# A two-layer encoder trunk: the second layer's memory keys and values move into that layer, and its mixer's input is transposed through DRAM

## The chip, the core and the metric

The kernel runs on one core of a Trainium2 chip. TensorE (PE in the profile) multiplies matrices; VectorE (DVE) and ScalarE (ACT) do the elementwise work and empty the accumulators; GpSimd (POOL) takes reciprocal square roots and a little setup; SyncE (SP) issues most transfers. Each engine works through its own list of instructions in the order in which the program was built, and waits where an instruction needs something that is not there yet. The metric is the time of the whole program in microseconds (us); lower is better.

## The reference

The input is one sequence of 256 frames with 1024 features, and a memory of 256 rows with 1024 features. Two layers follow each other. Each layer does the following in float32:

```
x = x + 1/2 * SwiGLU_1(RMSNorm(x))                      # FFN of 2816 units ("ffn 1")
h = RMSNorm(x);  q_s, k_s, v_s, q_m = split(h @ w_in)   # "mixer" begins
k_m, v_m = split(RMSNorm(mem) @ w_mem_kv)               # memory keys and values, 1024 -> 2*256
o_m = attention of q_m (4 heads of 64) over k_m, v_m
o_s = layer 0: chunked attention with a learned relative bias, 12 heads
      layer 1: differential attention with rotary positions, 6 heads
x = x + concat(o_s, o_m) @ w_out                        # mixer ends
x = x + 1/2 * SwiGLU_2(RMSNorm(x))                      # "ffn 2"
```

The memory keys and values of a layer depend on `mem` and on that layer's weights alone, not on `x`. So they can be made at any time before that layer's memory attention.

## The kernel before

Precision comes from a split: each float32 operand is written as hi + lo, where hi is the operand rounded to the matmul's input type, and a product is three matmuls (hi times hi, hi times lo, lo times hi) that add into one accumulator. The helper `dense` issues these three (L516, L519, L522). A weight chunk of 128x2048 comes from DRAM into one of 3 `raw` buffers; ScalarE casts it to `hi` in four pieces (L341), VectorE subtracts to get `lo` in four pieces (L359), and 4 pairs of hi and lo are held at a time. A chunk of the projection weights or of the memory weights then serves 24 matmuls of 512 columns.

The left operand has to be transposed, with features on partitions. Two ways are in the kernel. `prep_half` transposes four 128x128 blocks on TensorE (L552, tile `xtp`) and multiplies by the norm's gain out of the accumulator (L586). `prep_dram` uses none of TensorE: VectorE transposes 32x32 blocks (L597, `xb`), ScalarE's queue writes them to a DRAM scratch `xd` (L603) and reads them back in another order (L610, `xr4`), and VectorE multiplies by the gain (L616, `y`). Behind both, `prep_rest` casts on ScalarE (L624, `xh`) and subtracts on VectorE (L628, `xl`). This is done for two row blocks (tb) of 128 rows, in two halves (hf) of 512 features each. `finish` adds the accumulator to x (L668) and then starts one of the two ways; in the kernel before, only the end of ffn 1 in layer 0 takes the DRAM way.

The memory is transposed once, into a DRAM scratch `md`. `memory_prep` reads it back (L1043, four tiles `mr`) and makes, for each layer and each of 8 feature blocks kk, `memh` on ScalarE (L1106) and `meml` on VectorE (L1110, two instructions). `memory_kv` then multiplies these with `w_mem_kv` (tile `kv`, 48 matmuls for one layer), takes the head norm of the keys, and sends them through DRAM once more (`kd`, `kr`). In the kernel before, both layers' `memh`, `meml`, `kv` and their weights come at the start of layer 0's mixer: 96 matmuls stand between the last down projection of ffn 1 (tile `acc`) and the first input projection (tile `pj`).

What sets the order is a planner in the program, run when it is built. The class `Flow` holds a clock and the times at which it thinks that ScalarE, VectorE and GpSimd come free; each piece of work is a generator that yields a time or a condition. `split_hi` and `split_lo` go on when their engine is free within 0.4 us, or when their chunk is the one that TensorE is at (`calm_a`, `calm_v`). `memory_prep` goes on only where its engine is free at that very time:

```
yield lambda: flow.free["A"] <= flow.now
nc.scalar.activation(hi, src, AF.Copy, scale=g)
```

The planner's times are not measured ones; what it leaves is an order for each engine. The names in an order carry numbers, since a name such as `hi` has a new tile for every chunk.

Of the kernel before, what the change touches and what calls it, by code (L numbers as in the profile page):

```python
# [27 lines left out]
KT = D // P  # L28
# [6 lines left out]
GC_FFN1, GC_MIX, GC_MEM, GC_FFN2 = 0, 16, 32, 48  # L35
# [107 lines left out]
def kernel(  # L143
# [10 lines left out]
    nc = tc.nc  # L154
    PSUM = bass.MemoryType.PSUM
    NRAW, NHL, NT2 = 3, 4, 19
    flow = Flow()
# [12 lines left out]
    g4 = Slots(flow, gp, "g", 12)  # L170
# [44 lines left out]
    gcol = const.tile([P, NGC], F32, name="gcol")  # L215
# [67 lines left out]
    def add_chunk(parts, uses=8, w=1):  # L283
        return Item([add_raw(parts)], uses, w)
# [102 lines left out]
    plan = {}  # L387
# [102 lines left out]

    for l in range(DEPTH):
        plan_ffn(l, 1, ffn1_w_gate, ffn1_w_up, ffn1_w_down)
        if l == 0:
            for ll in range(DEPTH):
                plan[ll, "kv"] = [add_chunk(cols4(w_mem_kv[ll], c, 0, 512, 0)) for c in range(2)]
        plan[l, "in"] = []
        for blk in WI:
            ids = []
            for c in range(2):
                o, parts = 0, []  # L500
                for c0, n in blk:
# [184 lines left out]
    def ffn(l, nm, xt, gc_next):  # L686
# [251 lines left out]
        acc = Acc()  # L938
# [33 lines left out]
        for c in range(SPLIT):  # L972
            prog[0] = c
            if c in sv:
                if c == sv[0]:
                    flow.until(banks.has(4))
                    ms = [bank(f"m{j}", (P, 512)) for j in (1, 5, 6, 7)]
                t = seven(c, ms)
                if c == sv[-1]:
                    flow.spawn(seven_sums(ms, t))  # L980
                continue
            for k in range(2):
                for tb in range(2):
                    for hf in range(2):
                        down(c, k, tb, hf)
            g4.give()
            if (l, nm) == (0, 1) and c == 2:
                flow.spawn(memory_prep())
        if nm == 1:
            table_hint(AF.Exp)  # L990
        assert xt_room[0]
        xt_room[0] = False
        nxt = None if gc_next is None else Xt(nm == 2 and PAIR[l + 1, 1] is not None)
        for tb in range(2):
            flow.spawn(finish(acc, tb, nxt, gc_next, True, (l, nm) == (0, 1)))
# [34 lines left out]
    memT = {}  # L1030
# [55 lines left out]
        for tb in range(2):  # L1086
            yield from rsqrt(mrs[tb], s2[:, tb:tb + 1], 1, 1.0 / D)

    def memory_prep():
        yield lambda: len(memd) == 4 and g2.left >= 8  # L1090
        rs = []
        for q in range(4):
            rs.append(from_dram(memd[q], "mr"))
            yield flow.now + 1.0
        yield flow.now + 4.0
        for l in range(DEPTH):
            yield g4.has(4)
            mh, ml = ([g4.take([P, 4, SEQ], F32R, f"{n}{l}{i}") for i in range(2)] for n in ("memh", "meml"))
            tt = [None] * KT
            memT[l] = (mh, ml, tt)  # L1100
            for kk in range(KT):
                src = rs[kk // 2][:, :, :, kk % 2, :].rearrange("p a t j -> p t a j")
                g = gcol[:, GC_MEM + l * KT + kk:GC_MEM + l * KT + kk + 1]
                hi, lo = (m[kk // 4][:, kk % 4, :].rearrange("p (t a j) -> p t a j", t=2, a=4) for m in (mh, ml))
                yield lambda: flow.free["A"] <= flow.now
                nc.scalar.activation(hi, src, AF.Copy, scale=g)  # L1106
                yield flow.act(256)
                yield lambda: flow.free["V"] <= flow.now
                for tb in range(2):
                    nc.vector.scalar_tensor_tensor(out=lo[:, tb], in0=src[:, tb], scalar=g, in1=hi.bitcast(F32)[:, tb],  # L1110
                                                   op0=ALU.mult, op1=ALU.subtract)
                    tt[kk] = flow.dve(128, 0.06)
        g2.give(4)

    def split_evac(dst, src, gain):
# [186 lines left out]
    def mixer(l, xt, gc_next):  # L1302
# [518 lines left out]
```

## Time and profile before

| What | Value |
|---|---|
| Time, median of 3 runs (lowest to highest) | 950.66 us (949.93 to 950.89) |
| Span of the profiled execution, first to last instruction | 948.2 us |
| PE busy | 940.9 us, 99% of the span |
| VectorE, ScalarE, GpSimd busy | 828.6, 590.4, 110.0 us |
| Read from and written to DRAM | 190.04 and 15.20 MB |

The span lies 2.46 us under the median of the runs; the profile gives no other time of its own execution, so these 2.46 us stand for what lies around the span. A matmul's busy time runs to its modelled end and overlaps the next one's, so the distance between two starts is the number to use: 0.227 us for 128x512. In the timeline view a row gives start, length, engine, line, operation and names; equal rows that follow each other are merged, with x and their count.

### The profile page before, as it was taken

Reading aid. Unit: us, or ns where it says so; the run is one execution under the profiler, and the core shown is the slowest. Engines: PE = TensorE matmul, PEld = TensorE weight load, DVE = VectorE, ACT = ScalarE, POOL = GpSimd, SP = SyncE. Lnnn points to the kernel's source line nnn. Section 1 sums busy time; section 2 is a strip of 40 time slices with the busy share of each in tenths; the row PEclk is TensorE's granted clock in tenths of the full one; section 3 lists DMA queues with packets and bytes.
Section 4 is the critical chain, followed back from the end, with each engine's and each line's share of the span. In section 5 each row is a group of like instructions: output and inputs, shape, how many; then the busy total and the mean of one; then the engine's idle time right before and its main releaser. Section 6 shows DMA issues by size and latency. Waiting matters only on the chain. (4 is left out here: it accounts for less than half of the span.)

```text
span 948.2 us, 13317 instructions
## 1 busy us (share of the span) xinstructions
PE 940.9 (99%) x4456; PEld 772.1 (81%) x4456; DVE 828.6 (87%) x1501; ACT 590.4 (62%) x1126; POOL 110.0 (12%) x160
## 2 busy tenths in 40 slices
PE   9999999999999999999999999999999999999998
PEld 7888888887777888888888888888887788888887
DVE  6989988888787899989889899796989899998995
ACT  6656666677676756647546656563777765655671
POOL 1000038731210100000000000000434100000000
PEclk9999999999999999999999999999999999999999
DMA  9878799787525387887746679775632467589561
GB/s 296 271 229 252 227 332 307 244 268 250 178 90 178 106 258 224 266 285 219 244 146 216 224 222 295 241 248 166 216 119 82 133 215 229 183 258 331 175 226 48
DMA packets 172574, 206.13 MB, mean 217 GB/s; under 512 B 10265, under 2 KB 147290, under 8 KB 172506
## 3 DMA queue, kind: packets, MB, share of 16 engines
q1 hardware_dynamic: 169498, 202.92, 66.6%
q10 hardware_dynamic: 3008, 2.37, 0.8%
q8 instruction: 35, 0.57, 0.3%
q14 instruction: 33, 0.27, 0.1%
HBM read 190.04 MB, written 15.20 MB: 216 GB/s over the span
## 5 line engine op out<-in xcount | busy, mean ns | idle before, releaser
L341 ACT CAST hi<-raw 128x512 fp32r<-128x512 f32 (+1 forms) x466 | 335.1, 770 | 161.5 <-DMA raw<-in_ffn_w_up_dram 40.8
L359 DVE TENSOR_TENSOR lo<-raw,hi 128x512 fp32r<-128x512 f32 (+1 forms) x466 | 392.0, 875 | 32.9 <-ACT hi L341 32.6
L519 PE MATMUL gu<-lo,xh 128*128 128x512 f32 x528 | 205.5, 389 | 0.5 <-DVE lo L359 0.5
L522 PE MATMUL gu<-hi,xl 128*128 128x512 f32 x528 | 205.8, 390 | 0.0
L516 PE MATMUL gu<-hi,xh 128*128 128x512 f32 x528 | 205.6, 389 | 0.0
L522 PEld LDWEIGHTS gu<-hi,xl 128*128 128x128 f32 x528 | 99.1, 188 | 21.3 <-DVE xl L628 0.9
L519 PEld LDWEIGHTS gu<-lo,xh 128*128 128x128 f32 x528 | 99.1, 188 | 21.3 <-DVE lo L359 0.9
L516 PEld LDWEIGHTS gu<-hi,xh 128*128 128x128 f32 x528 | 99.1, 188 | 20.6 <-ACT xh L624 0.2
L522 PE MATMUL acc<-hi,ht 128*128 128x512 f32 x270 | 105.5, 391 | 0.0
L516 PE MATMUL acc<-hi,ht 128*128 128x512 f32 x270 | 105.1, 389 | 0.0
L519 PE MATMUL acc<-lo,ht 128*128 128x512 f32 x270 | 105.1, 389 | 0.0
L341 ACT CAST hi<-wsum 128x512 fp32r<-128x512 f32 x83 | 48.4, 619 | 32.7 <-DVE wsum L353 29.1
L519 PE MATMUL pj<-lo,xh 128*128 128x512 f32 x160 | 64.2, 401 | 0.0
L516 PE MATMUL pj<-hi,xh 128*128 128x512 f32 x160 | 63.8, 398 | 0.0
L522 PE MATMUL pj<-hi,xl 128*128 128x512 f32 x160 | 63.7, 398 | 0.0
L559 POOL TENSOR_TENSOR xr<-v,nhalf 128x1 f32<-128x1 f32 x12 | 10.7, 888 | 427.8 <-DVE v L557 427.8
L519 PEld LDWEIGHTS acc<-lo,ht 128*128 128x128 f32 x270 | 50.7, 188 | 10.5
L516 PEld LDWEIGHTS acc<-hi,ht 128*128 128x128 f32 x270 | 50.7, 188 | 10.4
L522 PEld LDWEIGHTS acc<-hi,ht 128*128 128x128 f32 x270 | 50.7, 188 | 10.4
L359 DVE TENSOR_TENSOR lo<-wsum,hi 128x512 fp32r<-128x512 f32 x83 | 53.6, 677 | 0.0
L702 ACT ACTIVATE sil<-gu,xr 128x256 f32<-128x256 f32 x72 | 33.8, 469 | 26.4 <-PE gu L522 24.8
L559 POOL TENSOR_TENSOR hf<-v,nhalf 128x8 f32<-128x8 f32 (+1 forms) x20 | 31.9, 1596 | 84.0 <-DVE v L557 74.9
(244 smaller groups left out, 1528.7 us busy)
## 6 DMA issues: line engine op xcount, KB each, us to landing
raw<-in_ffn_w_down_dram SPq DMA_DIRECT2D x176, 256.0 KB, 4.4
raw<-in_ffn_w_gate_dram SPq DMA_DIRECT2D x82, 512.0 KB, 4.6
raw<-in_ffn_w_up_dram SPq DMA_DIRECT2D x82, 512.0 KB, 5.2
raw<-in_w_in_dram SPq DMA_DIRECT2D x32, 512.0 KB, 5.1
hd<-hb SPq DMA_DIRECT2D x44, 256.0 KB, 4.8
hr<-hd SPq DMA_DIRECT2D x44, 256.0 KB, 5.0
raw<-in_w_out_dram SPq DMA_DIRECT2D x8, 1024.0 KB, 5.1
raw<-in_w_mem_kv_dram SPq DMA_DIRECT2D x4, 1024.0 KB, 8.8
```

The source lines that it names most:

```text
L341: nc.scalar.copy(out=it.part(0, q, w), in_=src())
L359: nc.vector.tensor_sub(it.part(1, q, w), src(), it.part(0, q, w).bitcast(F32))
L516: nc.tensor.matmul(out=ps, lhsT=xh, rhs=wh, start=start, stop=False)
L519: nc.tensor.matmul(out=ps, lhsT=xh, rhs=wl, start=False, stop=False)
L522: nc.tensor.matmul(out=ps, lhsT=xl, rhs=wh, start=False, stop=stop)
L559: nc.gpsimd.tensor_tensor(out=dst, in0=v[:, :n], in1=nhalf[:, :n], op=ALU.pow)
L702: nc.scalar.activation(sil, ps[tb][:, 0:256], AF.Silu, scale=xt.r[tb])
```

## The change

Two things are changed. First, `w_mem_kv` of layer 1 is loaded after ffn 1 of layer 1; `memory_prep` handles one layer, is started in each layer's ffn 1, and reads `md` back each time; and each mixer begins with its own layer's `memory_kv` (48 matmuls). Second, the end of ffn 1 takes the DRAM way (`prep_dram`) in both layers.

```diff
@@ plan
         plan_ffn(l, 1, ffn1_w_gate, ffn1_w_up, ffn1_w_down)
-        if l == 0:
-            for ll in range(DEPTH):
-                plan[ll, "kv"] = [add_chunk(cols4(w_mem_kv[ll], c, 0, 512, 0)) for c in range(2)]
+        plan[l, "kv"] = [add_chunk(cols4(w_mem_kv[l], c, 0, 512, 0)) for c in range(2)]
@@ ffn
-            if (l, nm) == (0, 1) and c == 2:
-                flow.spawn(memory_prep())
+            if nm == 1 and c == 2:
+                flow.spawn(memory_prep(l))
...
-            flow.spawn(finish(acc, tb, nxt, gc_next, True, (l, nm) == (0, 1)))
+            flow.spawn(finish(acc, tb, nxt, gc_next, True, nm == 1))
@@ memory
-    def memory_prep():
+    def memory_prep(l):
         yield lambda: len(memd) == 4 and g2.left >= 8
         rs = []
         for q in range(4):
             rs.append(from_dram(memd[q], "mr"))
             yield flow.now + 1.0
         yield flow.now + 4.0
-        for l in range(DEPTH):
-            yield g4.has(4)
...
+        yield g4.has(4)
...
         g2.give(4)
@@ mixer
-        if l == 0:
-            for ll in range(DEPTH):
-                memory_kv(ll)
+        memory_kv(l)
```

The body of `memory_prep`'s loop over layers stays as it was, one level further out. Over the whole program TensorE has 16 transposes fewer; VectorE has 4 block transposes more; ScalarE issues 8 transfers more and SyncE 4 more. Lines behind the first edit move up by two or three: L668 before is L666 after, L1110 is L1107.

**VectorE where layer 1's mixer begins.** The place is the addition of the last down accumulator of ffn 1, `x1<-acc11`, and what stands around it. Before:

```order
L668 SCALAR_TENSOR_TENSOR x1_86<-acc10_6096,x1_86 128x512
L628 TENSOR_TENSOR xl0_6484<-y_6585,xh0_6482 128x512
L586 TENSOR_TENSOR y_6608<-xtp_6599,gcol_103 128x512
L359 TENSOR_TENSOR lo127_0_6595<-raw118_6439,hi127_0_6594 128x512
L650 TENSOR_TENSOR sst_6615<-xss_6486 128x1
L557 TENSOR_SCALAR v_6617<-sst_6615 128x1
L359 TENSOR_TENSOR lo127_0_6595<-raw118_6439,hi127_0_6594 128x512 x2
L628 TENSOR_TENSOR xl1_6485<-y_6608,xh1_6483 128x512
L668 SCALAR_TENSOR_TENSOR x1_86<-acc11_6097,x1_86 128x512
L359 TENSOR_TENSOR lo127_0_6595<-raw118_6439,hi127_0_6594 128x512
L359 TENSOR_TENSOR lo128_0_6629<-raw119_6470,hi128_0_6628 128x512 x2
L586 TENSOR_TENSOR y_6668<-xtp_6656,gcol_103 128x512
```

With the change, from that addition on, in two pieces that follow each other:

```order
L666 SCALAR_TENSOR_TENSOR x1_86<-acc11_5958,x1_86 128x512
L359 TENSOR_TENSOR lo125_0_6476<-raw116_6317,hi125_0_6475 128x512
L595 STREAM_TRANSPOSE xb_6530<-x1_86 128x4x4x32
L359 TENSOR_TENSOR lo125_0_6476<-raw116_6317,hi125_0_6475 128x512
L614 TENSOR_TENSOR y_6488<-xr4_6486,gcol_103 128x512
L1107 SCALAR_TENSOR_TENSOR meml11_6221<-mr_6146,gcol_103,memh11_6219 128x128 x2
L359 TENSOR_TENSOR lo126_0_6500<-raw117_6348,hi126_0_6499 128x512
L648 TENSOR_TENSOR sst_6555<-xss_6372 128x1
L555 TENSOR_SCALAR v_6557<-sst_6555 128x1
L359 TENSOR_TENSOR lo126_0_6500<-raw117_6348,hi126_0_6499 128x512 x2
L626 TENSOR_TENSOR xl0_6369<-y_6488,xh0_6367 128x512
```

```order
L614 TENSOR_TENSOR y_6528<-xr4_6526,gcol_103 128x512
L359 TENSOR_TENSOR lo126_0_6500<-raw117_6348,hi126_0_6499 128x512
L359 TENSOR_TENSOR lo127_0_6538<-raw118_6481,hi127_0_6537 128x512
L626 TENSOR_TENSOR xl0_6369<-y_6528,xh0_6367 128x512
L1107 SCALAR_TENSOR_TENSOR meml11_6221<-mr_6156,gcol_103,memh11_6219 128x128 x2
L614 TENSOR_TENSOR y_6562<-xr4_6560,gcol_103 128x512
L359 TENSOR_TENSOR lo127_0_6538<-raw118_6481,hi127_0_6537 128x512 x3
L626 TENSOR_TENSOR xl1_6370<-y_6562,xh1_6368 128x512
L1107 SCALAR_TENSOR_TENSOR meml11_6221<-mr_6156,gcol_103,memh11_6219 128x128 x2
L614 TENSOR_TENSOR y_6580<-xr4_6578,gcol_103 128x512
L626 TENSOR_TENSOR xl1_6370<-y_6580,xh1_6368 128x512
```

`hi124`, `lo124`, `hi125`, `lo125` are layer 1's memory weights, `hi126` to `lo127` the first two chunks of its input projection. The three pairs of `meml11` here are feature blocks kk = 5, 6 and 7 of layer 1's memory, and they stand behind the addition of `acc11`; in the kernel before, all of them stand in layer 0.

**ScalarE at the same place.** Before, it casts weights and the transposed x (`hi128` and `hi129` are chunks of the second projection block):

```order
L341 CAST hi127_0_6594<-raw118_6439 128x512
L641 ACTIVATE junk_95,xss_6487<-x1_86 128x512
L341 CAST hi128_0_6628<-raw119_6470 128x512 x4
L341 CAST hi129_0_6663<-raw120_6573 128x512 x3
L624 CAST xh1_6483<-y_6668 128x512
```

With the change:

```order
L639 ACTIVATE junk_95,xss_6372<-x1_86 128x512
L601 DMA xd_6548<-xb_6530 128x512
L341 CAST hi127_0_6537<-raw118_6481 128x512
L622 CAST xh0_6367<-y_6488 128x512
L608 DMA xr4_6560<-xd_6516 128x4x128
L341 CAST hi127_0_6537<-raw118_6481 128x512 x2
L1103 ACTIVATE memh11_6219<-mr_6156,gcol_103 128x256
L622 CAST xh0_6367<-y_6528 128x512
L608 DMA xr4_6578<-xd_6548 128x4x128
L1103 ACTIVATE memh11_6219<-mr_6156,gcol_103 128x256
L622 CAST xh1_6368<-y_6562 128x512
```

The last two feature blocks of `memh11` stand among the transfers of the DRAM way, the last one behind the read of `xd_6548`, which holds the second half of x1.

**TensorE.** In layer 0's mixer 48 `kv` matmuls instead of 96 stand ahead of `pj`. In layer 1's mixer the first 24 `kv` matmuls (row block 0, three for each kk from 0 to 7) follow the last `acc` matmul at once, then 24 for row block 1, then `pj`; nothing stands between them.

More of the change, by code (lines that the diff above doesn't have):

```diff
@@ L1095, in memory_prep @@
         yield flow.now + 4.0
-        for l in range(DEPTH):
-            yield g4.has(4)
[L1098 to L1112, printed above, removed]
+        yield g4.has(4)
+        mh, ml = ([g4.take([P, 4, SEQ], F32R, f"{n}{l}{i}") for i in range(2)] for n in ("memh", "meml"))
+        tt = [None] * KT
+        memT[l] = (mh, ml, tt)
+        for kk in range(KT):
+            src = rs[kk // 2][:, :, :, kk % 2, :].rearrange("p a t j -> p t a j")
+            g = gcol[:, GC_MEM + l * KT + kk:GC_MEM + l * KT + kk + 1]
+            hi, lo = (m[kk // 4][:, kk % 4, :].rearrange("p (t a j) -> p t a j", t=2, a=4) for m in (mh, ml))
+            yield lambda: flow.free["A"] <= flow.now
+            nc.scalar.activation(hi, src, AF.Copy, scale=g)
+            yield flow.act(256)
+            yield lambda: flow.free["V"] <= flow.now
+            for tb in range(2):
+                nc.vector.scalar_tensor_tensor(out=lo[:, tb], in0=src[:, tb], scalar=g, in1=hi.bitcast(F32)[:, tb],
+                                               op0=ALU.mult, op1=ALU.subtract)
+                tt[kk] = flow.dve(128, 0.06)
         g2.give(4)
```

## The prediction

> **What bounds the kernel now.** I read the page's first part, then who TensorE waits for, then its order of time at the three places that the change touches.
>
> ```profile
> PE 940.9 (99%) x4456; PEld 772.1 (81%) x4456; DVE 828.6 (87%) x1501; ACT 590.4 (62%) x1126; POOL 110.0 (12%) x160
> PE qktp L552 <- DVE qkn L1023: 1.4, 1, 1.4
> PE warm L1749 <- POOL ident masks.py:199: 1.4, 1, 1.4
> PE gu L519 <- DVE lo L359: 0.5, 1, 0.5
> PE S L1461 <- ACT PT L1475: 0.2, 1, 0.2
> ```
>
> TensorE is busy 99% of the span, and all its waits over 0.15 us are these four, 3.5 us together; two belong to the start. So the time is what TensorE's list takes, back to back. The change can gain by taking instructions off that list, and by the 1.4 us at `qktp` in layer 0's mixer; it loses whatever wait it opens. VectorE at 87% is the next engine, and everything VectorE is asked to do within a short stretch has to be looked at.
>
> The last down matmuls before each mixer, and what follows them:
>
> ```profile
> 186.20 0.39 PE L522 MATMUL acc<-hi,ht 128*128 128x512 f32 x1
> 186.43 0.39 PE L516 MATMUL kv<-hi,memh 128*128 128x512 f32 x1
> 661.18 0.60 PE L552 MATMUL xtp<-ident,x 128*128 128x128 f32 x4
> 661.54 0.48 PE L522 MATMUL acc<-hi,ht 128*128 128x512 f32 x1
> 661.85 0.40 PE L516 MATMUL acc<-hi,ht 128*128 128x512 f32 x1
> 666.21 0.39 PE L522 MATMUL acc<-hi,ht 128*128 128x512 f32 x1
> 666.44 0.39 PE L516 MATMUL pj<-hi,xh 128*128 128x512 f32 x1
> ```
>
> Starts are 0.23 us apart (186.20 to 186.43; 0.227 over longer runs, which I use). Both mixers begin without a hole. In layer 1 the way over `xtp` is fully covered, so nothing is waiting there that the DRAM way could shorten.
>
> **Removed: 16 transposes on TensorE.** A group of four starts at 661.18, the next matmul at 661.54, and the one after it 0.31 later instead of 0.227. So a group costs 0.36 + 0.08 = 0.44 us, and four groups 1.8 us. These lie on TensorE's own list: minus 1.8.
>
> **Moved: 48 `kv` matmuls.** They leave layer 0's mixer and enter layer 1's; 48 x 0.227 = 10.9 us stay on the list. What changes is what they cover, at both ends.
>
> **Layer 0's mixer.** Call T the start of the first `kv` matmul, 186.43. Now `pj` starts at T + 10.9, its second row block at T + 16.3, and the second half of that at T + 19.1. The last of x in the kernel before:
>
> ```profile
> 199.87 0.68 DVE L628 TENSOR_TENSOR xl<-y,xh 128x512 fp32r<-128x512 f32 x1
> 204.44 0.62 ACT L624 CAST xh<-y 128x512 fp32r<-128x512 f32 x1
> 205.09 0.69 DVE L628 TENSOR_TENSOR xl<-y,xh 128x512 fp32r<-128x512 f32 x1 [0.84 <-ACT xh L624]
> ```
>
> The first half of row block 1 is there at 200.6 = T + 14.1, in time. The second half's `xh` ends at 205.06 = T + 18.6, against T + 19.1; its `xl` ends at 205.78 = T + 19.35, and is first read by the third matmul, at T + 19.5. The lists of VectorE and ScalarE up to there are almost unchanged. So the halved cover just suffices: I take 0.2 us. Bounds: 0 below, and above 1.5 if a read of `xd` lands as late as the slowest of the row quoted below.
>
> The 1.4 us at `qktp` may go or stay. Before, `qkn` stood on VectorE behind the memory keys of both layers; now 33 matmuls (7.5 us) lie between the end of its projection and its transposes instead of 30 (6.8 us), and square, sum, power and product have to fit in there. I take minus 0.5, between minus 1.4 and plus 1.
>
> **Layer 1's mixer: the term that decides.** Here T is the start of layer 1's first `kv` matmul. The 24th of them, for kk = 7, would start at T + 23 x 0.227 = T + 5.2. It reads `meml` of kk = 7. In VectorE's new list that stands behind the addition of `acc11`, which can only start when the last `acc` matmul is through, and 23 more instructions stand between the two. VectorE goes through them in order. Nearly the same sequence ran in layer 0's mixer before, and gives the steps:
>
> ```profile
> 186.63 0.69 DVE L668 SCALAR_TENSOR_TENSOR x<-acc,x 128x512 f32<-128x512 f32 x1
> 187.36 1.12 DVE L597 STREAM_TRANSPOSE xb<-x 128x512 f32<-128x512 f32 x1
> 188.40 0.65 DVE L359 TENSOR_TENSOR lo<-raw,hi 128x512 fp32r<-128x512 f32 x1
> 188.97 0.81 DVE L616 TENSOR_TENSOR y<-xr,gcol 128x512 f32<-128x512 f32 x1
> 189.70 1.32 DVE L359 TENSOR_TENSOR lo<-raw,hi 128x512 fp32r<-128x512 f32 x2
> 190.95 0.15 DVE L650 TENSOR_TENSOR sst<-xss 128x1 f32<-128x1 f32 x1
> 191.13 0.15 DVE L557 TENSOR_SCALAR v<-sst 128x1 f32<-128x1 f32 x1
> 191.20 0.68 DVE L359 TENSOR_TENSOR lo<-raw,hi 128x512 fp32r<-128x512 f32 x1
> 191.80 0.69 DVE L628 TENSOR_TENSOR xl<-y,xh 128x512 fp32r<-128x512 f32 x1
> 192.40 0.73 DVE L616 TENSOR_TENSOR y<-xr,gcol 128x512 f32<-128x512 f32 x1
> 193.05 0.68 DVE L359 TENSOR_TENSOR lo<-raw,hi 128x512 fp32r<-128x512 f32 x1
> L1110 DVE SCALAR_TENSOR_TENSOR meml<-mr,gcol,memh 128x128 fp32r<-128x128 f32 x32 | 10.2, 375 | 1.8 <-ACT memh L1106 1.8
> ```
>
> From start to start: the addition 0.73, `xb` 1.04, `lo` 0.60, `y` 0.69 (mean of 0.73 and 0.65), `xl` 0.60, the two small ones 0.25 together, `meml` 10.2 / 32 = 0.32. In the new list from `x1<-acc11` to the first `meml` of kk = 7: 0.73 + 1.04 + 10 x 0.60 (`lo`) + 3 x 0.69 (`y`) + 3 x 0.60 (`xl`) + 0.25 + 4 x 0.32 + 0.38 = 13.6. The addition started 0.2 after T, so that `meml` is there at T + 13.8. TensorE loses 13.8 - 5.2 = **8.6 us**.
>
> What could make it longer is ScalarE's queue and the transfers in it:
>
> ```profile
> DMA to landing us min/median/max: 2.2/3.1/5.7
> 189.81 0.62 ACT L624 CAST xh<-y 128x512 fp32r<-128x512 f32 x1 [0.40 <-DVE y L616]
> 189.88 0.38 ACTq L610 DMA_DIRECT2D xr<-xd  x1
> ```
>
> `memh` for kk = 7 stands on ScalarE behind the read of `xd_6548`, which waits for that write to land, and VectorE's third `y` waits for the read of `xd_6516`. That write goes out at about T + 0.8, behind casts that wait for the buffers that `acc11` frees; with 3.1 us for each leg and ScalarE's own work between, `xr4_6560` lands at about T + 8, and VectorE comes to it at T + 10. Covered by 2 us. With 5.7 for both legs it lands at about T + 12.2: 2 us more. So the wait lies between 8.6 and about 11; I take 8.6, which is VectorE's list without a single wait behind the addition, since the transfers have 2 us to spare. It is also the lower bound, as long as the list is worked through in order.
>
> After that wait the next things are ready: the second 24 `kv` take 5.4 us, and x of both row blocks is through VectorE 1.5 us after the wait ends.
>
> **Added and cheap.** `memory_prep` reads `md` again: four issues on SyncE of about 0.5 us, in the down part of ffn 1, behind which weight loads are queued that run up to three buffers ahead; if that cover is gone, 2 us.
>
> ```profile
> L1043 SPq DMA_DIRECT2D mr<-md x4: 359/513/653, 150.4 to 155.3; - x4
> 607.00:666.40 59.40, 59.40 (x269) 49.23 (x268) 49.90 (x88) 33.93 (x66) 0.34 (x1) 1.00 0.63 203
> 720.00:740.00 20.00, 19.68 (x119) 15.28 (x119) 19.05 (x50) 14.20 (x46) 7.62 (x7) 1.00 0.31 106
> ```
>
> VectorE gets ten of the sixteen `meml` ahead of T (3.2 us) and three `xb`, and loses two or three `y` there. The last two rows give, behind the length of the stretch, the busy time of PE, PEld, DVE, ACT and POOL: before the mixer VectorE has 9.5 us free of 59.4, so these fit: nothing. Later in layer 1's mixer VectorE is full (19.05 of 20) while TensorE has few holes; 8.6 us of standing still lets VectorE get ahead, which could give back up to 2 us. I take none.
>
> **Sum.** 948.2 - 1.8 + 0.2 - 0.5 + 8.6 = 954.7 for the span; with the 2.46 that lie between the span and the median, 957.2 us.
>
> **Rivals.**
>
> 1. *TensorE comes back slow from the wait.* The same groups at the start of the program:
>
> ```profile
> 1.36 2.50 PE L1749 MATMUL warm<-ident 128*128 128x128 f32 x10 [1.36 <-POOL ident masks.py:199]
> 3.88 1.11 PE L552 MATMUL xtp<-ident,x 128*128 128x128 f32 x4
> 6.31 0.60 PE L552 MATMUL xtp<-ident,x 128*128 128x128 f32 x4
> 0.00:5.00 5.00, 3.62 (x15) 3.00 (x15) 0.00 (x0) 1.90 (x3) 1.23 (x10) 1.00 0.58 187
> ```
>
> After idleness TensorE ran at half pace from 1.36 to about 6 us, some 4.6 us (four transposes took 1.11, later 0.60), though the stretch 0 to 5 shows a granted clock of 1.00. If the new wait does this, some 4.6 us of work take twice as long: 2.3 us more, 959.5. For it: TensorE then does about six matmuls in 9 us. Against it: by the same steps the wait comes in pieces of 2 to 3.5 us with matmuls between, and no stretch of this trace shows how long a pause may be. The Trainium skill, "TensorE: Matmul & The Clock Gate", Part 1 ("What's actually happening"), says that the clock falls to half after an idle window of about 3.4 us and needs as long of busy time to recover. By that figure, as an estimate, the loss would be 1.7 us; only the start agrees so far. Chance 0.2.
>
> 2. *The transfers decide* (ScalarE's queue, as above): wait 10.6, 959.2. Chance 0.1.
>
> 3. *Layer 1's mixer gives 2 us back*: 955.2. For it, VectorE's 19.05 of 20; against, TensorE has hardly a hole to close there. Chance 0.14.
>
> 4. *Faster: no wait.* If the list's order did not bind, for instance if `meml` were through before T, 8.6 falls away: 948.6. It would need VectorE to finish kk = 7 before `acc11`, against its list. Chance 0.05. *No change*: the wait about 2 us, because the 24th matmul tolerates more than I see. 951. Chance 0.04.
>
> Forecast 0.47: 957.2, itself good for 955.7 to 958.7. Range to hold 8 in 10: it reaches down over rival 3 and up over 1 and 2, 954.3 to 960.5. About 0.2% (1.9 us) is what a measurement of this kernel can tell from no change. By these cases: faster 0.05, same 0.04, slower 0.91.
>
> **What would show it.** TensorE's waits in the new trace: some 8 to 9 us at `kv` in layer 1's mixer, released by VectorE's `meml` (and ScalarE's `memh`), in two or three pieces, and none at `kv` in layer 0. Sixteen fewer `xtp`. `pj` of layer 0 within 0.5 us behind `kv`. Matmul starts 0.227 apart right behind the wait would speak against rival 1, 0.43 apart for it. A wait released by a transfer would be rival 2. I am wrong if `kv` in layer 1 runs through without a hole.

## The result: 964.3 us, 1.4% slower

| | before | after |
|---|---|---|
| Time, median (lowest to highest) | 950.77 us (949.93 to 951.18, 4 runs) | 964.30 us (963.37 to 964.83, 4 runs) |
| Ratio, with its 95% interval | 1 | 1.0139 (1.0127 to 1.0151) |
| Span of the profiled execution | 948.2 us | 961.5 us (its own time 963.37 us) |

The direction was predicted, the size was not: 957.2 us were forecast, with a range up to 960.5. The table sets the spans of the two profiled executions against each other by stage, from the start of one tile's first matmul to the next, and beside it what the prediction's sum had for that stage. The 10.9 us of moved `kv` matmuls are taken out on both sides. Of the four groups of transposes that are gone, three stood in ffn 1 and the last (669.16 in the profile before) behind the first `pj`, so the predicted 1.8 us are split over two stages.

| Stage | after minus before | predicted |
|---|---|---|
| start to the first down matmul (`acc`) of ffn 1 in layer 0 | +0.6 | 0 |
| layer 0's mixer | -0.3 | -0.3 |
| from there to the end of ffn 1 in layer 1 (12 transposes fewer) | -1.4 | -1.3 |
| first `kv` to first `pj` in layer 1, beyond 10.9 | +10.9 | +8.6 |
| layer 1's mixer, from `pj` to the first `gu` of ffn 2 (4 transposes fewer) | +3.4 | -0.4 |
| ffn 2 of layer 1 | +0.1 | 0 |
| sum (before rounding) | +13.3 | +6.5 |

The profile after, its first part and who TensorE waits for (total, times, longest):

```profile
PE 945.1 (98%) x4440; PEld 773.5 (80%) x4440; DVE 832.8 (87%) x1505; ACT 589.4 (61%) x1126; POOL 109.3 (11%) x160
PE kv L514 <- ACT memh L1103: 3.3, 1, 3.3
PE kv L520 <- DVE meml L1107: 3.1, 2, 2.0
PE xtp L550 <- DVE x L669: 1.7, 1, 1.7
...
PE qktp L550 <- DVE m L1364: 1.0, 2, 0.6
PE ptp L550 <- ACT PT L1472: 0.5, 1, 0.5
PE ptp L550 <- DVE pe L1520: 0.4, 1, 0.4
PE qmtp L550 <- ACT pe L1506: 0.3, 1, 0.3
...
```

Sixteen matmuls are gone from TensorE's list (4456 to 4440). In their place stand three waits at `kv`, and below them a row of small ones, most of them in layer 1's mixer (the one behind L1520 lies in layer 0's), that the kernel before did not have. Its 1.4 us at `qktp <- qkn` is gone. TensorE's order of time at the start of layer 1's mixer:

```profile
654.39 0.39 PE L514 MATMUL kv<-hi,memh 128*128 128x512 f32 x1
...
658.40 0.50 PE L520 MATMUL kv<-hi,meml 128*128 128x512 f32 x1
662.22 0.79 PE L514 MATMUL kv<-hi,memh 128*128 128x512 f32 x1 [3.32 <-ACT memh L1103]
662.81 0.63 PE L517 MATMUL kv<-lo,memh 128*128 128x512 f32 x1
664.60 0.80 PE L520 MATMUL kv<-hi,meml 128*128 128x512 f32 x1 [1.16 <-DVE meml L1107]
665.52 0.80 PE L514 MATMUL kv<-hi,memh 128*128 128x512 f32 x1
666.11 0.63 PE L517 MATMUL kv<-lo,memh 128*128 128x512 f32 x1
668.71 0.80 PE L520 MATMUL kv<-hi,meml 128*128 128x512 f32 x1 [1.97 <-DVE meml L1107]
669.30 0.63 PE L514 MATMUL kv<-hi,memh 128*128 128x512 f32 x1
669.73 0.63 PE L517 MATMUL kv<-lo,memh 128*128 128x512 f32 x1
...
672.54 0.39 PE L520 MATMUL kv<-hi,meml 128*128 128x512 f32 x1
```

T is 654.39. The 24th matmul was due at T + 5.2 and started at 668.71 = T + 14.3: **9.1 us** of waiting. From there to `pj` (676.17) 25 matmuls took 7.46 us instead of 25 x 0.227 = 5.68: **1.8 us** more, since they start 0.43 apart until 672.3 and 0.227 apart only then. The granted clock (the number behind the five engines' busy times) is halved for just that stretch:

```profile
654.39:662.06 7.67, 4.51 (x19) 3.19 (x17) 6.92 (x14) 5.98 (x14) 0.83 (x1) 1.00 1.05 321
662.06:672.30 10.24, 6.83 (x14) 4.11 (x15) 6.65 (x14) 1.85 (x4) 0.00 (x0) 0.50 0.87 280
672.29:676.17 3.88, 3.88 (x18) 3.20 (x17) 2.25 (x6) 3.10 (x6) 1.39 (x1) 1.00 0.10 36
```

VectorE's list from the addition of the last accumulator to the last `meml`, the stretch that the prediction had worked out, and two of ScalarE's instructions in that time:

```profile
654.60 0.69 DVE L666 SCALAR_TENSOR_TENSOR x<-acc,x 128x512 f32<-128x512 f32 x1 [0.33 <-PE acc L520]
...
655.80 1.10 DVE L595 STREAM_TRANSPOSE xb<-x 128x512 f32<-128x512 f32 x1
...
658.01 0.60 DVE L1107 SCALAR_TENSOR_TENSOR meml<-mr,gcol,memh 128x128 fp32r<-128x128 f32 x2
...
659.72 0.16 DVE L648 TENSOR_TENSOR sst<-xss 128x1 f32<-128x1 f32 x1 [0.51 <-ACT junk L639]
...
664.20 0.61 DVE L1107 SCALAR_TENSOR_TENSOR meml<-mr,gcol,memh 128x128 fp32r<-128x128 f32 x2
665.29 0.69 DVE L614 TENSOR_TENSOR y<-xr,gcol 128x512 f32<-128x512 f32 x1 [0.49 <-DMA xr<-xd]
...
668.31 0.61 DVE L1107 SCALAR_TENSOR_TENSOR meml<-mr,gcol,memh 128x128 fp32r<-128x128 f32 x2
```

```profile
658.44 0.62 ACT L341 CAST hi<-raw 128x512 fp32r<-128x512 f32 x1 [1.69 <-DMA raw<-in_w_in_dram]
...
661.66 0.51 ACT L1103 ACTIVATE memh<-mr,gcol 128x256 fp32r<-128x256 f32 x1
```

From the addition to the end of the first `meml` of kk = 7 (about 668.65) it took 14.05 us, and the third matmul of kk = 7 starts right behind. The sum of steps gave 13.6 us with no idle time. Measured are 13.05 us of steps and two idle times of 0.51 and 0.49 us: the steps were priced a little too long, and that hid half of the idle time. ScalarE's `memh` of kk = 6, which ends the first piece of the wait, stands behind a cast that waited 1.69 us for a weight transfer; no run takes that wait alone away.

### The profile page after: what moved, and what is told of

Read it like the earlier page. It is cut to its first block, busy times and chain, and to the rows that moved or that the text cites. A ratio compares the mean times of both kernels' runs of the same rounds, so it can differ in the third digit from the quotient of the medians.

```text
span 961.5 us, 13305 instructions
## 1 busy us (share of the span) xinstructions
PE 945.1 (98%) x4440; PEld 773.5 (80%) x4440; DVE 832.8 (87%) x1505; ACT 589.4 (61%) x1126; POOL 109.3 (11%) x160
## 4 chain that ended last, share of the span: by engine, by line
PE 90%; DVE 5%; DMA 2%; ACT 2%; issue 1%; SPq 0%; ACTq 0%
PE gu L517 13%; PE gu L520 13%; PE gu L514 12%; PE acc L514 8%; PE acc L517 8%; PE acc L520 8%; PE pair_m L517 3%; PE pair_m L520 3%; PE pair_m L514 3%; PE gu L537 2%; PE pj L520 2%; PE pj L514 2%; PE pj L517 2%; DVE lo L359 2%; PE gu L543 1%; PE ptp L550 1%
```

## Experiments

Two theories stood at the start. The first was the prediction's: the loss at `kv` is the place of `memh` and `meml` in the lists of ScalarE and VectorE, behind the x that now goes through them. The other was that one of the two parts costs this by itself. The 3.4 us inside the mixer had no theory yet. All ratios below are to the kernel before, timed beside each set (medians of 950.2 to 950.3 us).

### Each part alone

Memory work of layer 1 in its own mixer, x by TensorE:

```diff
-            flow.spawn(finish(acc, tb, nxt, gc_next, True, nm == 1))
+            flow.spawn(finish(acc, tb, nxt, gc_next, True, (l, nm) == (0, 1)))
```

> The memory keys and values of layer 1 are made in layer 1's own mixer, as in the change; x of that mixer is transposed by TensorE, as before. In the new list of VectorE all `meml` of layer 1 stand nine or more entries ahead of the addition `x1<-acc11`. Theory A (the wait at `kv` is the place of `meml` in VectorE's list, and it stands so late because the x that goes by VectorE and DRAM takes the free places): no wait over 0.5 us at `kv`, granted clock 1.00 throughout, 951 us within 1, or up to 954 if the 3 us that the end of layer 1's mixer lost in the change come with the memory work itself. Rival B (the move of the memory work alone makes the wait, since ffn 1 has no room for it): 8 to 11 us of wait at `kv`, 962 to 964 us.

x through DRAM in both layers, all memory work in layer 0 as before:

```diff
-            flow.spawn(finish(acc, tb, nxt, gc_next, True, (l, nm) == (0, 1)))
+            flow.spawn(finish(acc, tb, nxt, gc_next, True, nm == 1))
```

> x of layer 1's mixer goes by VectorE and DRAM as in the change, the memory keys and values of both layers stay in layer 0's mixer. Theory A (the DRAM way needs a cover of 48 `kv` matmuls): its second row block is there at T + 14 to T + 19 after the last `acc` matmul (as in layer 0), and `pj` wants it at T + 5.4 and T + 8.2, so TensorE waits 9 to 11 us at `pj` in layer 1, and if the granted clock falls to half after that, 2 us more: 950.8 - 1.8 + 9 to 13 = 958 to 962 us. Rival B (the DRAM way is cheap, and the loss comes from the memory work alone): 949 us, 1.8 less than before.

The memory work alone: 952.90 us, ratio 1.0025 (1.0016 to 1.0034). Nothing waits at `kv` and the clock stays at 1.00: the last `meml` starts at 653.2, where the first `kv` starts at 656.4. So rival B fell. The remaining +2.7 us lie inside the mixers of both layers.

The DRAM way alone: 960.14 us, ratio 1.0099 (1.0085 to 1.0112), within 958 to 962 as expected, but with a shorter wait than I wrote. TensorE's order of time there, and the granted clock behind the wait:

```profile
670.02 0.80 PE L516 MATMUL pj<-hi,xh 128*128 128x512 f32 x1 [5.22 <-ACT xh L624]
...
671.70 0.79 PE L522 MATMUL pj<-hi,xl 128*128 128x512 f32 x1 [0.46 <-DVE xl L628]
667.00:673.57 6.57, 3.09 (x6) 1.99 (x7) 5.97 (x13) 3.93 (x8) 0.83 (x1) 0.50 0.90 307
```

5.4 us at one place instead of 9 to 11, then half clock again for the first six matmuls, and the rest in smaller waits further on. What follows: the DRAM way needs the cover of `kv`, and by itself the moved memory work is far from costing 13 us. The two hurt each other: what the DRAM way puts on VectorE pushes `meml` from ahead of the products to behind them.

### The splitting of the memory is allowed to keep up

```diff
-            yield lambda: flow.free["A"] <= flow.now
+            yield lambda: flow.free["A"] <= flow.now + SLACK
...
-            yield lambda: flow.free["V"] <= flow.now
+            yield lambda: flow.free["V"] <= flow.now + SLACK
```

> The change, and the splitting of the memory for layer 1 may go on as soon as ScalarE or VectorE are at most 0.4 us behind, like the other users of this limit, instead of only when they are idle. All `meml` now stand 23 or more entries of VectorE's list ahead of `x1<-acc11`. Theory A (the 10.9 us at `kv` are the late place of `memh` and `meml`, and the half clock that follows the wait): no wait over 0.5 us at `kv`, no stretch of half clock, 964.3 - 10.9 = 953.4 us with the end of layer 1's mixer as in the change; 950 us if that end also closes up; 949 if all of it does. Rival B (transfers decide, the x of layer 1 is late whatever the place of `meml`): the wait moves to `pj` in layer 1 and 5 us or more of it stay, 958 us or more.

951.56 us, ratio 1.0011 (1.0002 to 1.0020); later again on another chip (it stands beside the kernels without key work below) 951.71 us, 1.0017 (1.0008 to 1.0026). Two words in the planner's condition take 12.7 us off the change. The stretch from the first `kv` to the first `pj`, and the group of `meml` with its first and last start:

```profile
655.42:666.30 10.88, 10.88 (x49) 9.01 (x48) 9.34 (x18) 6.66 (x15) 2.22 (x2) 1.00 0.91 281
L1107 DVE SCALAR_TENSOR_TENSOR meml<-mr,gcol,memh x32: 334/340/429, 157.6 to 633.7; 128x128 fp32r<-128x128 f32 x32
```

48 matmuls in 10.88 us, at full clock: no hole. The last `meml` starts 21.7 us ahead of the first `kv` matmul; in the change it started 14.2 us behind it. So the 10.9 us are shown to be the place of `memh` and `meml`, and what follows from it. The transfers were not the limit: with `meml` early, no wait of 5 us appears at `pj` (rival B).

With this the table of the two parts is complete (median, ratio):

| | x by TensorE | x through DRAM |
|---|---|---|
| all `kv` in layer 0 | before, 950.2, 1 | 960.1, 1.0099 |
| `kv` in its own layer | 952.9, 1.0025 | the change, 964.3, 1.0139 |
| the same, with slack | 954.3, 1.0042 (below) | 951.6, 1.0011 |

None of the variants beats the kernel before.

### The clock after the wait

The waits at `kv` are filled with matmuls on the identity that nothing reads; all other instructions keep their places. `mid` puts them between the second and the third matmul of a product.

```diff
...
+    def fill(bank_, n):
+        for _ in range(n):
+            nc.tensor.matmul(out=bank_[:, 0:P], lhsT=ident, rhs=ident, start=True, stop=True)
...
+                    if (l, tb) == (1, 0) and kk == 6:
+                        fill(ps[1], 30)
+                        mid = (ps[1], 14)
+                    if (l, tb) == (1, 0) and kk == 7:
+                        mid = (ps[1], 22)
```

> The change, with 66 matmuls of 128 columns on the identity put into the three waits of TensorE at `kv` in layer 1 (30, 14 and 22; each takes some 0.11 us at full clock, so 3.3, 1.5 and 2.4 us, less than the wait they stand in); they write a bank that is overwritten afterwards, and every other instruction stands where it stood. Theory A (part of the loss is that TensorE's clock is halved after the wait): the granted clock stays 1.00, the 24 matmuls of the second row block are 0.227 us apart instead of 0.43, and the kernel takes about 2.3 us less, 962.0 us. Rival B (the matmuls after the wait are slow for another reason, their operands or the transfers): no gain, 964.3 us, or more if the fillers overrun.

968.05 us, 1.0182: slower than the change by some 4 us, because I had mis-sized the fillers. One of them took 0.22 us and not 0.11 (each of these matmuls of float32 operands stands in the trace as two instructions, x60 for the first 30), so they overran the waits. The clock did stay at 1.00. With about half as many:

```diff
-                        fill(ps[1], 30)
+                        fill(ps[1], 14)
-                        mid = (ps[1], 14)
+                        mid = (ps[1], 6)
-                        mid = (ps[1], 22)
+                        mid = (ps[1], 11)
```

> As the kernel before it, with 31 fillers instead of 66 (14, 6 and 11): a matmul of 128 columns on the identity took 0.22 us there, not 0.11, so the first set overran the waits. Now 3.1, 1.3 and 2.4 us stand in waits of 3.6, 1.6 and 2.4. Theory A (the clock): `meml` of kk = 7 still sets the end of the wait, at T + 14.3; after it the rest is 0.227 us apart from the start, where in the change it was 0.43 apart from 668.7 to 672.3, so 1.7 us less, 962.6 us (between 962.0 and 963.0), granted clock 1.00. Rival B: no gain, 964.3 us.

962.49 us, 1.0124 (1.0109 to 1.0140), against 1.0139 of the change: 1.8 us less at the medians, as expected (962.6), and 1.4 us by the ratios; the two intervals overlap, so the trace has to carry it:

```profile
665.98 2.62 PE L528 MATMUL kv<-ident 128*128 128x128 f32 x22
668.63 0.50 PE L522 MATMUL kv<-hi,meml 128*128 128x512 f32 x1
668.96 0.39 PE L514 MATMUL kv<-hi,memh 128*128 128x512 f32 x1
669.19 0.40 PE L517 MATMUL kv<-lo,memh 128*128 128x512 f32 x1
...
674.43 0.39 PE L514 MATMUL pj<-hi,xh 128*128 128x512 f32 x1
662.06:672.30 10.24, 9.50 (x56) 7.95 (x56) 6.83 (x14) 1.81 (x4) 0.00 (x0) 1.00 0.88 284
```

The last `meml` is no earlier (its matmul at 668.63, against 668.71), but the matmuls behind it are 0.23 apart at once, and `pj` comes 5.80 us later instead of 7.46. Same operands, same transfers, same place: only TensorE's idleness differs. So the rest of the loss at `kv` is the halved clock.

This profiled execution was the slowest of the four (963.93 us, the others 961.53 to 962.70 at a clock of 1.00). It lost its gain again further on: behind a wait of 1.9 us its clock was halved for 3.4 us.

```profile
PE qktp L556 <- DVE m L1376: 1.9, 1, 1.9
692.04:695.45 3.41, 3.41 (x11) 2.83 (x12) 3.41 (x8) 2.04 (x5) 2.21 (x2) 0.50 0.85 267
```

### The 3.4 us inside layer 1's mixer

From the first `pj` to the first `gu` of ffn 2, in the kernel before and in the change:

```profile
666.44:769.84 103.40, 102.96 (x580) 82.85 (x578) 93.96 (x203) 73.68 (x196) 32.24 (x28) 1.00 0.46 151
```

```profile
676.17:783.01 106.84, 103.06 (x575) 82.22 (x574) 95.46 (x207) 71.42 (x193) 32.67 (x28) 1.00 0.45 143
```

TensorE's busy time is the same, so it is 3.4 us of small waits at full clock, behind the `kv` stretch. Two profiles of one program, the kernel with the slack, had 105.8 and 107.2 us in this stage, so single profiles that differ here by 1.5 us or less decide nothing. Theory C was that VectorE's work on the memory keys, now in this mixer, stands ahead of what TensorE waits for. Three kernels with the slack tested it: most of that work left out; x by TensorE; and that work only where VectorE has room.

```diff
-            nat = yield from head_norm(ps[:, 0:256], 4, mrs[tb], "kmn")
+            if l == 1:
...
+                nat = g2.take([P, 256], F32, "kmn")
+                nc.scalar.activation(nat, ps[:, 0:256], AF.Copy, scale=mrs[tb])
...
+                if l == 1:
+                    nc.scalar.activation(lo, src, AF.Copy, scale=g)
...
+                    continue
```

> The change with the 0.4 us of slack for the splitting, and with most of VectorE's work on layer 1's memory keys left out: they are not normalised (a copy by ScalarE in place of square, sum, power and product) and the low part of the keys is a copy by ScalarE in place of four VectorE instructions. Some 4.2 us of VectorE's 162.4 in that stretch go, ScalarE gets about as much as it had. Theory C (what is left of the loss, some 2.4 us inside layer 1's mixer, is VectorE: the memory keys stand on it ahead of `qkn`, `m` and `pe`, which TensorE waits for): the waits at `qktp` and `ptp` shrink by 1 to 2 us, 949.5 to 950.5 us. Rival D (the order of the units or the banks, whatever VectorE does): 951.5 us, waits as they were.

> The slack for the splitting, the memory work of layer 1 in its own mixer, but x of that mixer by TensorE as before. Against the kernel with slack and x by DRAM (951.6 us) it has 16 transposes more (1.8 us), and four `xb` of 1.04 us less on VectorE. Theory C (VectorE is what the mixer waits for): the 1.8 us are partly given back by shorter waits, 951.5 to 953 us. Rival D (the DRAM way of x costs nothing there): 953.4 us, exactly 1.8 more.

```diff
+            yield lambda: l == 0 or flow.free["V"] <= flow.now + SLACK
             t = turn_blocks(kb[0][:, :, tb], nat)
...
+                yield lambda: l == 0 or flow.free["V"] <= flow.now + SLACK
                 for j in range(2):
                     nc.vector.scalar_tensor_tensor(out=lo[:, j], ...
```

> The slack for the splitting, x by DRAM, and in layer 1 the transposes and the low part of the memory keys go to VectorE only when it is at most 0.4 us behind; nothing is left out. Theory C: 3.4 us of VectorE's work move behind `qkn` and `m` at the start of the mixer, the waits at `qktp` fall by 1 us or more, 950.5 us; it is the memory unit that then comes later, and if outproj waits for it the gain is lost. Rival D: 951.5 us.

Light keys: 951.41 us, 1.0012, no gain. x by TensorE: 954.28 us, 1.0042 (1.0030 to 1.0055), 2.7 us above the kernel with slack where 1.8 was the most I expected from the transposes. Calm: 952.97 us, 1.0025, worse by 1.4. Theory C missed in all three. Rival D came in the first alone; the second is also above its 953.4 us, and the third above its 951.5.

The three did show something else. In the kernel before, the units of attention in layer 1 follow each other in one order at the end; in the change, in the light one and in the one with x by TensorE, the memory's first `S<-km` stands 5 to 7 us ahead of the last ordinary unit. The wait at `xtp` of 1.7 us came with this order in the change and with x by TensorE. That became theory F, with one rule:

```diff
                 yield lambda: qm[1][tb] is not None and all(v is not None for r in kvres[l][2] for v in r)
+                yield lambda: l == 0 or (2, 1) in started
...
+            started.add((c, tb))
```

> The change, and in layer 1 the attention of the memory (`S<-km`) may only begin once the last unit of the ordinary heads (`S<-k,q` of row block 1) has begun. In the kernel before, and in the two kernels of the first set where the end of the mixer was shorter, that unit came first; in the change the first memory unit stands 7 us ahead of it, and its `otp` then ends the mixer 1.7 us late, behind the addition `x` on VectorE. Theory F (this order of the units costs the mixer's end about 2 us, whatever happened at `kv`): the wait at `xtp` goes, 964.3 - 1.9 = 962.4 us, layer 1's mixer from `pj` to `gu` 105 us instead of 106.8. Rival G (the order only shows a lateness that VectorE has anyway): the wait moves to another place, 964.3 us within 0.5. The wait at `kv` and the half clock stay as in the change in both.

> The same rule for the units, in the kernel with the slack for the splitting and x by TensorE (954.3 us), whose mixer 1 reads like that of the change from `pj` on (106.9 us against 106.8). Theory F: 954.3 - 1.9 = 952.4 us. Rival G: 954.3 us within 0.5.

> The same rule for the units, in the kernel with the slack, x by DRAM, and most of VectorE's work on layer 1's memory keys left out (no normalisation, the low part a copy by ScalarE). There the order of the units was that of the change, in the kernel with the work (951.6 us) it was that of before, so the two were not comparable; now they are. Theory C (what is left of the loss is VectorE's work on the memory keys at the start of the mixer): 949.5 to 950.2 us, layer 1's mixer from `pj` to `gu` at most 104.3 us against 105.8. Rival D (it is not VectorE's): 951.5 us, 105.8 us. Theory F for this kernel alone: 951.4 - 1.7 = 949.7 us.

> The change with the slack for the splitting and the rule for the units, and the low part of layer 1's memory keys made by ScalarE and GpSimd (a scaling in place, then a subtraction) instead of four instructions of VectorE; nothing is left out. It takes 2.1 us from VectorE at the place where `m` and `qkn` wait behind them, and gives GpSimd, which is busy 12% there, some 4 us. Theory C: 951.6 - 0.5 to 1 = 950.8 us. Rival D, or GpSimd's own `hf` behind it late: 951.6 us or more.

The last of the four also moves four instructions of layer 1 to other engines:

```diff
+                if l == 1:
+                    for j in range(2):
+                        full = r[:, :, j, pr, :]
+                        nc.scalar.activation(full, full, AF.Copy, scale=g)
...
+                        nc.gpsimd.tensor_sub(lo[:, j], full, hi.bitcast(F32)[:, j])
...
+                    continue
```

The change with the rule: 963.50 us, 1.0145 (1.0131 to 1.0159), as without it. The wait left `xtp` and came back at another place:

```profile
PE qmtp L550 <- ACT pe L1571: 1.8, 1, 1.8
PE qktp L550 <- DVE m L1364: 1.0, 2, 0.6
```

That is rival G: the order showed a lateness and did not make it. x by TensorE with the rule: 953.26 us, 1.0037, between what F and G expected and a change inside the intervals. The light keys, now in the same order as the kernel with slack: 950.93 us, 1.0011 (1.0002 to 1.0020), the same ratio as with the work in. Its profiled execution had 104.0 us from `pj` to `gu`, which theory C had asked for, but the medians give 0.6 us at most. Keys by GpSimd: 952.78 us, 1.0034, worse. (GpSimd is busy 31% of this mixer in the kernel with the slack, 32.66 us of 105.77; the 12% are its share of the whole span before.)

Then all work on layer 1's keys behind the products was left out, with the slack and in the change, both with the rule:

```diff
+            if l == 1:
+                for i in range(2):
+                    nc.scalar.activation(km[:, i, tb, :], ps[:, 0:256], AF.Copy, scale=mrs[tb])
...
+                nc.scalar.activation(vm[:, tb, :], ps[:, 256:512], AF.Copy, scale=mrs[tb])
...
+                banks.give()
+                return
```

> The kernel with the slack for the splitting, and all work on layer 1's memory keys behind the products left out: no norm, no transposes, no way through DRAM; ScalarE copies the products into the buffers of keys and values (six instructions, as many as it had), VectorE and GpSimd do nothing for them. The 48 products stay. Theory H (the work on the memory keys, on VectorE, GpSimd and in its two transfers, is what layer 1's mixer loses once it is made there): from `pj` to `gu` 103.5 to 104 us instead of 105.8, and about 2 us less than the kernel with slack on the same chip, 949.5 us. Rival I (the mixer takes longer whatever becomes of the keys, for instance because x arrives later and its row blocks closer together): 105 us or more, at most 0.7 us less.

> The same work left out in the change with the rule for the units (963.5 us). The wait at `kv` and the half clock stay as they are. Theory H: from `pj` to `gu` 103.5 to 104.5 us instead of 106.5, 961.0 us. Rival I: 106 us or more, 963 us.

> The kernel with the slack for the splitting again (951.6 us before), on the chip of the two kernels without the work on the keys, as what the first of them is compared with. The time should be 951.5 within 0.7 us; the comparison goes by the ratios to the kernel before.

With the slack: 951.84 us without the work, 951.71 us with it, on the same chip (1.0018 against 1.0017). In the change: 963.20 us, 1.0132 (1.0119 to 1.0145), against 963.50 with it. Theory H fell, for the slack kernel clearly, and rival I had the times right; the reason that I named with it, a later x, is not shown by that. The profile of the second one could have misled:

```profile
675.97:780.26 104.29, 102.88 (x576) 82.74 (x574) 89.10 (x192) 69.48 (x188) 31.64 (x26) 1.00 0.44 142
```

104.3 us is what H had said, but this one execution took 960.64 us while the other three took 962.65 to 964.09.

In the first 35 us of the mixer VectorE is as full without the work on the keys as with it, and the splits of weights have grown from 24 to 26 between 666 and 700 (the kernel with slack first, the one without key work second):

```profile
664.87:699.87 35.00, 31.55 (x154) 24.55 (x153) 31.41 (x62) 22.02 (x50) 8.99 (x7) 1.00 0.68 219
L359 DVE TENSOR_TENSOR lo<-raw,hi 128x512 fp32r<-128x512 f32 x24 | 16.0, 702 | 0.0
```

```profile
665.21:700.21 35.00, 33.15 (x162) 25.94 (x161) 31.50 (x61) 24.07 (x59) 8.94 (x7) 1.00 0.69 219
L359 DVE TENSOR_TENSOR lo<-raw,hi 128x512 fp32r<-128x512 f32 x26 | 17.4, 706 | 0.8 <-ACT hi L341 0.8
```

So the last question was whether these splits are early and in the way. Two kernels held them back at the mixer's start, with -0.6 as below and with -0.2 (`room` is `SLACK` everywhere else):

```diff
-        return lambda: flow.free["V"] <= flow.now + SLACK or i <= at[0] + AHEAD
+        return lambda: flow.free["V"] <= flow.now + room[0] or i <= at[0] + AHEAD
...
+        if l == 1:
+            room[0] = -0.6
...
+        room[0] = SLACK
         proj(3, qk_evac(2))
```

> The kernel with the slack for the splitting of the memory, and from the start of layer 1's mixer to its third projection the splits of weights on VectorE (`lo`) are only placed where VectorE has been free for 0.6 us, unless a product is due that needs them; before and after that they may fill it up to 0.4 us behind, as always. Nothing is left out. Theory J (TensorE waits at `pj` for `xl` and at `qktp` for `m` because splits that are not yet needed stand ahead of them): these waits, 0.9 to 1.3 and 1.8 us in the kernel with the slack, shrink to less than 1 us together, 949.5 to 950.5 us against 951.6. Rival K (VectorE has no room to shift anything to, the splits come late in their turn): the waits at `qktp` turn into waits at `pj` or `acc` for `lo`, 951.6 us or more.

> The same with 0.2 us in place of 0.6: fewer splits are moved. Theory J: between the kernel with the slack and the one with 0.6, 950 to 951 us. Rival K: 951.6 us or more; if only the larger amount comes too late for the splits, this one is the faster of the two.

962.20 us (1.0123) and 957.89 us (1.0080). Rival K, and strongly: with 0.6 us, TensorE waits for the very splits that were held back, and the waits at `qktp` are as long as ever. The longest wait halved the clock as well, for 6.8 us:

```profile
PE pj L519 <- DVE lo L361: 4.4, 4, 3.4
PE qktp L552 <- DVE m L1366: 1.9, 4, 0.7
```

So these splits were not early enough to be put off even by 0.2 us. **Still open:** what the 1.5 to 4 us inside layer 1's mixer come from. Shown is that they are not the order of the units, and not the work on the memory keys, and that they appear with x by either way once `kv` is made there. With x through DRAM they appear even where `kv` stays in layer 0: that kernel also waits 1.2 us at `qktp` for `m`. VectorE is nearly full in that stretch, but in the kernel before it is just as full (31.02 us of 35, the row below) without TensorE waiting, so its load alone does not explain them. One rival was not tested: in the kernel with the slack ScalarE's casts wait 6.6 us for weight transfers in the first 35 us of this mixer, against 1.1 in the kernel before. In the change they do not wait there at all, so this can be no more than a part. I have no run that names the instructions.

```profile
666.44:701.44 35.00, 35.00 (x176) 28.51 (x175) 31.02 (x65) 25.02 (x62) 10.63 (x10) 1.00 0.58 187
```

## Why the prediction was right or wrong

- **The term that decides, 8.6 us at `kv`, was right.** Place and releaser came as worked out: `meml` of kk = 7 at T + 14.3 against 13.8, the loss 9.1 us. The kernel with slack shows the cause by taking it away. Its three pieces also came, the first released by ScalarE's `memh`. That the size is so close is partly luck: 1.0 us of idle time that the sum did not have stood against steps priced 0.55 us too long.
- **Rival 1 was not a rival but the next term of the sum.** I gave the halved clock 0.2 and left it out of the forecast, because "the wait comes in pieces of 2 to 3.5 us with matmuls between". That reason did not hold. The first piece alone, 3.8 us from start to start (658.40 to 662.22) and 3.3 us of it idle, was enough, and in the kernel with half the fillers one wait of 1.9 us was. The halved clock cost 1.8 us in the trace, and 1.4 to 1.8 us less time came out when the waits were filled; I had priced it at 2.3 from the program's start. By the figure of the Trainium skill, "TensorE: Matmul & The Clock Gate", Part 1 ("What's actually happening"), the estimate had been 1.7 us, and the 1.8 us of the trace agree.
- **The step that failed is "Later in layer 1's mixer ... I take none".** Its only bound was a gain of up to 2 us (rival 3, chance 0.14), from VectorE getting ahead while TensorE stood still. The stage lost 3.4 us, and 3.8 against the sum, which has 0.4 us of removed transposes there. That is the largest miss: by itself it takes 957.2 to 961.0, above the range. In place of the gain the runs showed small waits of TensorE at `xtp`, `qktp`, `ptp` and `qmtp`, 3.7 us together against 0.2 before. Their cause stays open. VectorE was no busier than before (31.10 us against 31.02 in the first 35), and taking work off it gained nothing that could be measured; so the row with 19.05 us of 20 was no ground for a forecast in either direction, and the term needed a bound on the side of a loss.
- **Layer 0's number was right by luck.** `pj` followed `kv` there with no hole (predicted: 0.2 us), and the whole 1.4 us at `qktp` went (predicted: 0.5). That would have given 1.4 us; the mixer gave 0.3. New waits took 0.7 us of it (0.4 at `ptp`, 0.3 at `S`), and two profiles of the kernel with the slack differ by 0.9 us in this stage.
- **The transposes** gave 1.4 us in ffn 1, where three of the four groups stood and 1.3 were predicted. The fourth stood in layer 1's mixer, where its 0.4 us cannot be told from the loss.
- **Rival 2 (the transfers)** was not the limit, but nearer to it than "2 us to spare". Between 653 and 676 us the writes to `xd` took 5.7 us at the median to land and the reads 6.7, not 3.1. The third `y` started at T + 10.9, after 0.5 us of idleness, where the prediction had it at T + 10. Rivals 3 and 4 did not happen.

8.6 + 2.3 (0.5 in VectorE's list, 1.8 of clock) + 3.8 (mixer) + 0.6 (start) + 0.1 (ffn 2) - 2.1 (the predicted terms of -1.8 and -0.3) = 13.3. The start term is no effect of the change: the same program with slack started 0.5 us late in one execution and not at all in another.

## What to carry to other kernels

Work that is moved to cover one engine has inputs made by others: look where those stand in their own lists, and what else the same change puts there. Here each part alone cost 0.3% or 1.0%, both together 1.4%, and a slack of 0.4 us in the rule that places the inputs brought that to 0.1%. Where a predicted wait has pieces of about 2 us or more, put the halved clock behind it into the sum or at least into the range: here one of 1.9 us brought it, and one of 1.7 us did not. And where the next engine is nearly full, give "nothing changes later" a bound on the side of a loss.

## What the runs showed of the hardware

The granted clock fell to half in the profiles of four kernels, and again in the two variants of the change at the change's own place:

| Kernel | TensorE idle before or during the fall | Half clock | Length |
|---|---|---|---|
| the change | 658.90 to 662.22, 3.3 us | 662.06 to 672.30 | 10.2 us |
| DRAM way alone | 664.81 to 670.02, 5.2 us | 666.89 to 673.71 | 6.8 us |
| 31 fillers | 690.00 to 691.91, 1.9 us | 692.04 to 695.45 | 3.4 us |
| splits held back by 0.6 us | 668.70 to 672.12, 3.4 us | 671.42 to 678.25 | 6.8 us |

It fell 3.2 us into the wait in the change, 2.1 us into it with the DRAM way alone, and behind a wait of only 1.9 us with the fillers. The 1.7 us at `xtp` in the change left it at 1.00. In the change it held through the pauses with two or three matmuls between them, and then until 3.6 us after matmuls had begun to follow each other again. The Trainium skill, "TensorE: Matmul & The Clock Gate", Part 1 ("What's actually happening"), counts in free-running windows of 3.413 us; the four lengths agree with three, two, one and two of them. That the clock falls after a whole idle window, as the prediction had it from the same section, the second and third row do not bear out.

Matmuls that nothing reads kept the clock at 1.00 through the waits at `kv` (662.06 to 672.30), at no cost as long as they ended ahead of the data: the matmul behind the last of them started at 668.63, against 668.71 in the change.
